# Gate half of a gMLP projection: four seven-product pairs per group, two low parts made by an accumulating DMA

## The chip, the cores and the metric

The kernel runs on one core of a Trainium2 chip. The time is the device time of one execution in microseconds (us). Four of the core's engines matter here: TensorE (PE in the profile) for matmuls, VectorE (DVE) and ScalarE (ACT) for elementwise work, and GpSimd (POOL). SyncE (SP) has a queue from which DMAs are issued; POOL has one too. Each engine runs its own instructions in a fixed order and waits on semaphores for the others.

## The reference

The reference is a two-layer trunk on an input of 256 rows by 2048 columns in float32: a gated MLP mixer (gMLP), a feed-forward part, a latent attention, another feed-forward part, each followed by a layer norm. The change lies in the first matmul of the first mixer, in the half of its columns that becomes `v`:

```python
z = jax.nn.gelu(x @ w_in)          # x: 256 x 2048, w_in: 2048 x 12288
u, v = jnp.split(z, 2, axis=-1)    # v: 256 x 6144
v = layer_norm(v, ln_g, ln_b)
```

## The kernel before

**High and low parts.** Every float32 operand is split into two tiles of a matmul format of reduced precision (`F32R`): a high part, the operand rounded to that format, and a low part, what is left. A product of two operands then takes three matmuls: high by high, low by high, and high by low (`prod_b`, L280). The high part of a weight is a cast on ACT, the low part a subtraction on DVE (L104 and L105, or `_cast`, L111, with L112 and L113).

**Groups and pairs.** The `v` half (loop at L593) computes 6144 columns in six groups of 1024. A group goes through the 2048 rows of the weight in eight pairs of 128-row blocks. The weights of one pair and one group are a chunk: a tile of 128 partitions by 2048 floats (1 MB), loaded by one DMA from SP (`_load`, L75). The 256 rows of `x` are two blocks as well, so a pair is a 2 x 2 by 2 x 2 block product, with blocks of 512 columns.

- An ordinary pair (`Banks.eight`, L337) makes the eight block products, 8 x 3 = 24 matmuls with 512 columns. Its chunk is of the kind "wide": one cast and one subtraction, 2048 wide each.
- A seven-product pair (`Banks.seven`, L344) uses a scheme with seven block products of sums of blocks, 21 matmuls. Its chunk is of the kind "seven" (`_seven`, L115): three sums on DVE (tile `ts`, L119, one instruction 1024 wide and two 512 wide), then casts and subtractions for the weight (`wh`, `wl`, 1536 wide) and for the sums (`th`, `tl`, 1536 and 512 wide). The sums of `x` (tile `xc`) are made once, by `combine` (L206) during group 0, which has wide pairs alone, and kept for the groups after.

Which pair comes when and which is of which kind stands in `V_PAIRS` and `V_SEVEN` (L49 and L50). Groups 1 to 5 have three seven-product pairs each, 2, 3 and 4, at positions 1, 4 and 6 of the group's order (positions count from 0).

**End of a group.** Four of the sums of a seven-product group lie in banks of their own. After the last seven-product pair `rest` (L354) folds them: a copy of bank p1 on ACT (L359), then u, u3, w and d on DVE (L360 to L363). After the group's last pair four additions (L616) join them with the other four banks, four gelus on ACT follow (L617), and, in the group after, four squares for the statistics of the layer norm (L590).

**Feed and order.** `Feed` hands the chunks out in order. Each `next` (L139) first calls `ahead` (L131), which splits chunks until two beyond the one asked for are split, and loads two further ones. All chunk tiles, raw ones and parts, live in one pool of 22 buffers of 8 KB per partition ("big", L152); a tile's first instruction waits until the last user of its buffer is done. The `v` tiles of finished groups, the parts of `x` and two tiles with the `xc` are in the same pool. The program text gives only the dependencies and a priority: when the kernel is built, a scheduler lays down the order of the instructions on each engine and which buffer each tile gets. That order can be read from the built program, of the kernel before and of the changed one.

Of the kernel before, what the change touches and what calls it, by code (L numbers as in the profile page):

```python
# [12 lines left out]
ALU = mybir.AluOpType  # L13
# [32 lines left out]

V_PAIRS = [[0, 1, 2, 3, 4, 5, 6, 7]] + [[0, 2, 1, 5, 3, 6, 4, 7]] * 5  # L49
V_SEVEN = [()] + [(2, 3, 4)] * 5  # L50


def halves(n_k):
# [12 lines left out]
class Feed:  # L66
# [24 lines left out]
    def _split(self):  # L91
        i = self.split
        cols, kind = self.chunks[i][1:]
        raw = self.raw.pop(i)
        if kind == "seven":
            self.parts[i] = self._seven(i, raw)
            self.split += 1
            return
        hi = self.pool.tile([P, 2048], F32R, tag="big", name=f"wh{i}")
        lo = self.pool.tile([P, 2048], F32R, tag="big", name=f"wl{i}")  # L100
        step = 512 if i == 0 else cols if kind == "wide" and i > 2 else 1024 if cols == 2048 else cols // 2
        for o in range(0, cols, step):
            c = slice(o, o + step)
            self.nc.scalar.copy(hi[:, c], raw[:, c])  # L104
            self.nc.vector.tensor_tensor(lo[:, c], raw[:, c], hi[:, c].bitcast(F32), ALU.subtract)  # L105
            if i == 0 and o == step:
                self.between[1]()
        self.parts[i] = (hi, lo)
        self.split += 1
# [20 lines left out]

    def ahead(self, n_load, n_split):  # L131
        while self.split < min(n_split, len(self.chunks)):
            if self.loaded == self.split:
                self._load()
            self._split()
        while self.loaded < min(n_load, len(self.chunks)):
            self._load()
# [9 lines left out]
def trunk(ctx: ExitStack, tc: tile.TileContext, x, xT, gm_in, gm_wout, ffn_up, ffn_dn,  # L147
# [19 lines left out]
    chunks = []  # L167
    n_up = ffn_up.shape[1]
    for g in range(6):
        for p in V_PAIRS[g]:  # L170
            chunks.append((gm_in[8 * g + p], 2048, "seven" if p in V_SEVEN[g] else "wide"))
    chunks += [(gm_in[i], 2048, "") for i in range(48, gm_in.shape[0])]

    def back(w, n_k):
# [101 lines left out]
    def x_parts(xs, k, b):  # L276
        t = xs[k // 4]
        return (t[:, k % 4, b * P : (b + 1) * P], t[:, k % 4, S + b * P : S + (b + 1) * P])
# [314 lines left out]
    for gi in range(6):  # L593

        acc = Banks(f"v{gi}", DIRECT if gi == 0 else DIRECT + OWN if gi % 2 else OWN + DIRECT)
        rest = (None,) * 4
        for c, p in enumerate(V_PAIRS[gi]):
            a = [[x_parts(xhl, 2 * p + j, b) for j in range(2)] for b in range(2)]
            got = feed.next()
            if p in V_SEVEN[gi]:  # L600
                acc.seven(a, xc[p], *got)
                if p == V_SEVEN[gi][-1]:
                    rest = acc.rest()
            else:
                acc.eight(a, *got)
            if gi == 0 and p in V_SEVEN[1]:
                x4 = xraw[p // 2]
# [70 lines left out]
    for gi in range(12):  # L678
        acc = [bank(f"u{gi}_{f}") for f in range(4)]
        for c in range(4):  # L680
            hi, lo = feed.next()
# [136 lines left out]
    for c in range(6):  # L818
        hi, lo = feed.next()
# [33 lines left out]
    for c in range(2):  # L853
        hi, lo = feed.next()
# [109 lines left out]
    for hf in range(2):  # L964
        acc = [[bank(f"vv{hf}_{b}_{f}") for f in range(2)] for b in range(2)]
        for c in range(2):
            hi, lo = feed.next()
# [20 lines left out]
    for t in range(3, H + LAG):  # L988
        k = t - LAG
        if k >= 0:  # L990
            if k % 2 == 0:
                hi, lo = feed.next()
# [22 lines left out]
    for c in range(8):  # L1015
        left = 7 - c
        hi, lo = feed.next(splits=2 if left > 5 else 3 if left > 2 else 4, loads=2 if left > 2 else 1)
# [107 lines left out]
```

## Time and profile before

| | |
|---|---|
| time, median of 3 runs | 2501.7 us (2501.2 to 2503.17) |
| the profiled execution | 2504.94 us, with a span of 2503.2 us from first to last instruction |
| granted TensorE clock of that execution | 0.997 |

In the rows of the profile "us" are microseconds; a line such as L105 is that of the kernel before. Tile names are given without their numbers. In a row of a timeline the two first numbers are the start and the length, and brackets at the end hold the idle time of the engine just ahead of the instruction and what ended it. PE matmuls are pipelined: a row's length is longer than the step from one matmul to the next, so the step is taken from pieces of the chain of several matmuls.

### The profile page before, as it was taken

The page shows a single profiled execution, that of the slowest core. Times are in us where ns is not written, and L with a number is a line of the kernel's source. Part 1 is how long each engine was busy: PE and PEld are TensorE (multiplying, and loading weights), DVE is VectorE, ACT ScalarE, POOL GpSimd, SP SyncE. Part 2 cuts the span into 40 slices and gives each one's busy share as a digit, 9 for nine tenths or more (in the row PEclk, how much of TensorE's full clock was granted, in tenths as well). Part 3 has the DMA queues.
Part 4 walks back from the last instruction along what each step waited for, and adds up shares of the span by engine and source line. Part 5 has one row for each costly group of instructions (what it writes and reads, how often), then busy time and mean ns, then how long its engine had stood idle before and what let it go on. Part 6 is the DMA issues. An engine that isn't in the chain of part 4 may idle for free.

```text
span 2503.2 us, 32484 instructions
## 1 busy us (share of the span) xinstructions
PE 2484.7 (99%) x13066; PEld 2138.5 (85%) x13066; DVE 1840.0 (74%) x2439; ACT 1335.0 (53%) x1763; POOL 2.9 (0%) x17
## 2 busy tenths in 40 slices
PE   9999999999999999999999999999999999999998
PEld 7888888888887888888888888988888888888886
DVE  6887866678787767666778887756686676668796
ACT  6565644445464546545655564565365555546553
POOL 0000000000000000000000000000000000000000
PEclk9999999999999999999999999999999999999999
DMA  7555554556566555555546674444555455555654
GB/s 276 214 190 202 202 177 161 184 192 204 187 207 252 188 182 202 185 180 176 195 156 202 217 269 157 156 143 178 183 205 183 165 206 178 182 180 172 214 203 168
DMA packets 86310, 480.19 MB, mean 192 GB/s; under 512 B 7696, under 2 KB 8336, under 8 KB 46608
## 3 DMA queue, kind: packets, MB, share of 16 engines
q1 hardware_dynamic: 86160, 478.13, 54.2%
q8 instruction: 102, 1.67, 0.3%
q14 instruction: 48, 0.39, 0.0%
HBM read 476.00 MB, written 2.10 MB: 191 GB/s over the span
## 4 chain that ended last, share of the span: by engine, by line
PE 98%; DVE 1%; ACT 0%; DMA 0%; issue 0%; SPq 0%; DVEq 0%; ACTq 0%
PE up L164 36%; PE u L164 11%; PE dn_q L164 9%; PE dn_p L164 6%; PE v_q L164 5%; PE wo_q L164 5%; PE v_p L164 3%; PE mo L164 3%; PE dn_e L164 3%; PE wo_p L164 3%; PE wo_e L164 2%; PE upf L164 2%; PE v_e L164 2%; PE mkv L164 1%; PE qn L164 1%; PE kn L164 1%
## 5 line engine op out<-in xcount | busy, mean ns | idle before, releaser
L105 DVE TENSOR_TENSOR wl<-raw,wh 128x1024 fp32r<-128x1024 f32 (+3 forms) x664 | 929.3, 1424 | 218.7 <-ACT wh L104 161.4
L104 ACT CAST wh<-raw 128x1024 fp32r<-128x1024 f32 (+3 forms) x664 | 786.4, 1215 | 341.1 <-DVE wl L105 125.2
L164 PE MATMUL up<-xhl,wh 128*128 128x512 f32 x2624 | 610.7, 390 | 0.0
L164 PEld LDWEIGHTS up<-xhl,wh 128*128 128x128 f32 x2624 | 487.4, 188 | 97.7
L164 PEld LDWEIGHTS up<-xhl,wl 128*128 128x128 f32 x2624 | 325.8, 192 | 6.4
L164 PE MATMUL up<-xhl,wl 128*128 128x256 f32 x2624 | 328.1, 283 | 0.0
L164 PE MATMUL u<-xhl,wh 128*128 128x512 f32 x768 | 183.8, 393 | 0.3 <-DVE h_u L309 0.2
L164 PEld LDWEIGHTS u<-xhl,wh 128*128 128x128 f32 x768 | 141.3, 188 | 30.8 <-PE s L164 2.1
L112 ACT CAST th<-ts 128x1536 fp32r<-128x1536 f32 x90 | 93.0, 1052 | 113.7 <-DVE ts L119 84.1
L113 DVE TENSOR_TENSOR tl<-ts,th 128x1536 fp32r<-128x1536 f32 x90 | 106.5, 1219 | 13.1 <-ACT th L112 12.2
L164 PEld LDWEIGHTS u<-xhl,wl 128*128 128x128 f32 x768 | 95.6, 192 | 2.0
L164 PE MATMUL u<-xhl,wl 128*128 128x256 f32 x768 | 96.7, 283 | 0.0
L112 ACT CAST wh<-raw 128x1536 fp32r<-128x1536 f32 x45 | 66.7, 1482 | 46.9 <-DMA raw<-in_ffn_dn_dram 13.2
L164 PE MATMUL wo_q<-wh,woa 128*128 128x512 f32 x288 | 88.9, 389 | 0.0
L113 DVE TENSOR_TENSOR wl<-raw,wh 128x1536 fp32r<-128x1536 f32 x45 | 78.8, 1752 | 6.3 <-PE dn_q L164 2.8
L164 PE MATMUL mo<-wh,oT 128*128 128x512 f32 x256 | 82.8, 404 | 0.0
L164 PE MATMUL v_q<-wh,xhl 128*128 128x512 f32 x264 | 82.0, 392 | 0.0
L164 PE MATMUL dn_q<-wh,dn0a 128*128 128x512 f32 x248 | 76.5, 389 | 0.0
L164 PE MATMUL dn_q<-wh,dn1a 128*128 128x512 f32 x248 | 76.3, 389 | 0.0
L309 DVE TENSOR_TENSOR h_0a<-up,lo_0a 128x256 f32<-128x256 f32 x41 | 17.2, 420 | 74.2 <-ACT lo_0a L307 74.1
L309 DVE TENSOR_TENSOR h_1a<-up,lo_1a 128x256 f32<-128x256 f32 x41 | 17.2, 420 | 73.3 <-ACT lo_1a L307 73.3
L164 PEld LDWEIGHTS wo_q<-wh,woa 128*128 128x128 f32 x288 | 54.1, 188 | 11.2
(490 smaller groups left out, 3847.7 us busy)
## 6 DMA issues: line engine op xcount, KB each, us to landing
raw<-in_ffn_up_dram SPq DMA_DIRECT2D x172, 1024.0 KB, 4.7
raw<-in_gm_in_dram SPq DMA_DIRECT2D x93, 1024.0 KB, 4.7
raw<-in_ffn_dn_dram SPq DMA_DIRECT2D x84, 1024.0 KB, 5.3
raw<-in_gm_wout_dram SPq DMA_DIRECT2D x48, 1024.0 KB, 5.3
raw<-in_ml_out_dram SPq DMA_DIRECT2D x16, 1024.0 KB, 4.8
raw<-in_ml_b_dram SPq DMA_DIRECT2D x14, 1024.0 KB, 4.8
raw<-in_ml_kv_dram SPq DMA_DIRECT2D x5, 864.0 KB, 4.4
lng<-in_ln_rows_dram SPq DMA_DIRECT2D x4, 1024.0 KB, 8.6
```

Source lines behind the costliest of these rows:

```text
L104: self.nc.scalar.copy(hi[:, c], raw[:, c])
L105: self.nc.vector.tensor_tensor(lo[:, c], raw[:, c], hi[:, c].bitcast(F32), ALU.subtract)
L112: self.nc.scalar.copy(hi, raw)
L113: self.nc.vector.tensor_tensor(lo, raw, hi.bitcast(F32), ALU.subtract)
L164: nc.tensor.matmul(o, l, r, start=start, stop=stop, skip_group_check=True)
L309: nc.vector.tensor_tensor(h, acc[:, 0:S], lo, ALU.add)
```

## The change

In groups 1 to 5 a fourth pair, 5, becomes a seven-product pair, and pairs 1 and 6 get a new kind, "low"; the order of the pairs changes, so that seven-product pairs stand at positions 1, 3, 5 and 6, "low" ones at positions 2 and 4 and wide ones at 0 and 7. For a "low" chunk ACT writes the negated and rounded weight into the low tile; a DMA issued from POOL then adds the weight, read from memory again, to that tile, which leaves the low part; ACT casts the high part as before. The pair itself is an ordinary one with 24 matmuls. `ahead` splits a "low" chunk one chunk earlier than it otherwise would. Lines after the inserted ones move by 10 to 15.

```diff
-V_PAIRS = [[0, 1, 2, 3, 4, 5, 6, 7]] + [[0, 2, 1, 5, 3, 6, 4, 7]] * 5
-V_SEVEN = [()] + [(2, 3, 4)] * 5
+V_PAIRS = [[0, 1, 2, 3, 4, 5, 6, 7]] + [[0, 2, 1, 3, 6, 4, 5, 7]] * 5
+V_SEVEN = [()] + [(2, 3, 4, 5)] * 5
+V_LOW = [()] + [(1, 6)] * 5
...
         hi = self.pool.tile([P, 2048], F32R, tag="big", name=f"wh{i}")
         lo = self.pool.tile([P, 2048], F32R, tag="big", name=f"wl{i}")
+        if kind == "low":
+
+            self.nc.scalar.mul(lo, raw, -1.0)
+            self.nc.gpsimd.dma_start(lo, self.chunks[i][0], accum_op=ALU.add)
+            self.nc.scalar.copy(hi, raw)
+            self.parts[i] = (hi, lo)
+            self.split += 1
+            return
...
             if self.loaded == self.split:
                 self._load()
             self._split()
+
+        if self.split < len(self.chunks) and self.chunks[self.split][2] == "low":
+            if self.loaded == self.split:
+                self._load()
+            self._split()
...
         for p in V_PAIRS[g]:
-            chunks.append((gm_in[8 * g + p], 2048, "seven" if p in V_SEVEN[g] else "wide"))
+            chunks.append((gm_in[8 * g + p], 2048, "seven" if p in V_SEVEN[g] else "low" if p in V_LOW[g] else "wide"))
```

## The prediction

> **What bounds the kernel now.** I read the page first: its busy times, the chain of work that ended last, and the issues of DMAs.
>
> ```profile
> span 2503.2 us, 32484 instructions
> ...
> PE 2484.7 (99%) x13066; PEld 2138.5 (85%) x13066; DVE 1840.0 (74%) x2439; ACT 1335.0 (53%) x1763; POOL 2.9 (0%) x17
> ...
> PE 98%; DVE 1%; ACT 0%; DMA 0%; issue 0%; SPq 0%; DVEq 0%; ACTq 0%
> ...
> raw<-in_gm_in_dram SPq DMA_DIRECT2D x93, 1024.0 KB, 4.7
> ...
> lng<-in_ln_rows_dram SPq DMA_DIRECT2D x4, 1024.0 KB, 8.6
> ```
>
> TensorE sets the end: 98% of the chain is PE. So a matmul removed is time removed, as long as every weight part is in place when PE asks for it. The change touches groups 1 to 5 of the gate half alone, so the second view is the chain in order of time there, cut to two of its pieces, and the third the busy times of two groups (columns: length, then busy us of PE, PEld, DVE, ACT, POOL, the granted clock, DMA share, GB/s).
>
> ```profile
> 88.05 2.04 PE v_q L164 x9
> ...
> 129.53 2.04 PE v_q L164 x9
> ```
>
> ```profile
> 94.00:135.50 41.50, 41.50 (x185) 34.37 (x184) 36.42 (x33) 26.76 (x32) 0.00 (x0) 1.00 0.56 203
> 135.50:177.00 41.50, 41.50 (x185) 34.38 (x184) 36.98 (x35) 26.67 (x35) 0.00 (x0) 1.00 0.58 203
> ```
>
> Nine matmuls in 2.04 us are 0.2267 us each. The same piece returns after 41.48 us, and a group has 5 wide pairs of 24 matmuls and 3 seven-product pairs of 21: 183 x 0.2267 = 41.48. PE never waits here. But DVE is busy 36.4 to 37.0 of 41.5 us: whatever is put off on DVE has little room to be caught up. How much lead DVE has is the fourth view, its instructions in order of time around the end of a group.
>
> ```profile
> 86.80 0.69 DVE L360 TENSOR_TENSOR v1u<-v_p,v1p 128x512 f32<-128x512 f32 x1 [3.98 <-PE v_p L164]
> 87.40 1.22 DVE L119 TENSOR_TENSOR ts<-raw 128x1024 f32<-128x1024 f32 x1
> 88.54 0.68 DVE L361 TENSOR_TENSOR v1w<-v_q,v1u 128x512 f32<-128x512 f32 x1
> 89.14 0.68 DVE L362 TENSOR_TENSOR v1u<-v_p,v1u 128x512 f32<-128x512 f32 x1
> 89.73 0.68 DVE L363 TENSOR_TENSOR v1d<-v1w,v_p 128x512 f32<-128x512 f32 x1
> 90.33 0.68 DVE L119 TENSOR_TENSOR ts<-ts,raw 128x512 f32<-128x512 f32 x1
> 90.93 1.75 DVE L113 TENSOR_TENSOR wl<-raw,wh 128x1536 fp32r<-128x1536 f32 x1
> ...
> 93.20 2.35 DVE L113 TENSOR_TENSOR tl<-ts,th 128x1536 fp32r<-128x1536 f32 x2
> ...
> 100.65 2.29 DVE L105 TENSOR_TENSOR wl<-raw,wh 128x2048 fp32r<-128x2048 f32 x1 [0.51 <-ACT wh L104]
> 102.86 1.22 DVE L119 TENSOR_TENSOR ts<-raw 128x1024 f32<-128x1024 f32 x1
> ```
>
> At 86.80 DVE reaches the fold of the last seven-product pair (v1u) and has idled 3.98 us for PE: by then the low parts of the next two wide pairs are done. That idle time is the lead.
>
> **The change part by part.** Positions 0 to 7 are the eight pairs of a group in their order; seven-product pairs now stand at 1, 3, 5, 6, pairs with a DMA-made low part at 2 and 4, wide ones at 0 and 7.
>
> Removed on PE: one pair per group goes from 24 to 21 matmuls, 3 x 0.2267 = 0.68 us, in five groups 3.4 us (the built program has 15 matmuls fewer). This is all that PE can gain, 0.14% of the time. About 0.2%, 5 us, is what a measurement of this kernel can tell from no change.
>
> DVE, per group: a seven-product pair costs 1.22 + 2 x 0.68 + 1.75 + 2.35 = 6.7 us against 2.29 for a wide one, so +4.4; two subtractions of 2.29 go. The load stays near 37 us of a shorter group. For ACT I read its instructions in order of time.
>
> ```profile
> 91.05 1.49 ACT L112 CAST th<-ts 128x1536 fp32r<-128x1536 f32 x1 [4.40 <-DVE ts L119]
> 93.32 0.62 ACT L112 CAST th<-ts 128x512 fp32r<-128x512 f32 x1 [0.78 <-DVE ts L119]
> 93.84 1.92 ACT L104 CAST wh<-raw 128x2048 fp32r<-128x2048 f32 x1
> 96.25 0.63 ACT L617 ACTIVATE v<-v 128x512 f32<-128x512 f32 x1 [0.49 <-DVE v L616]
> ...
> 98.72 1.90 ACT L104 CAST wh<-raw 128x2048 fp32r<-128x2048 f32 x1
> 100.53 0.72 ACT L590 ACTIVATE vsq<-v,vc 128x512 f32<-128x512 f32 x1
> ...
> 102.65 0.71 ACT L590 ACTIVATE vsq<-v,vc 128x512 f32<-128x512 f32 x1
> ...
> 103.36 1.47 ACT L112 CAST wh<-raw 128x1536 fp32r<-128x1536 f32 x1
> 104.89 2.00 ACT L112 CAST th<-ts 128x1536 fp32r<-128x1536 f32 x2
> ```
>
> ACT, per group: the seven-product pair takes 1.47 + 2.00 = 3.5 against 1.9, +1.6, and the two negations take 1.9 each (as a cast of that shape): 26.7 + 5.4 = 32 of 40.8 us. No engine is over its time; what counts is the order.
>
> Moved: the order of instructions in the built kernels. Before, DVE subtracts the low parts of positions 7 and 0 ahead of the fold. After, its order is: fold u, low part of 7, folds w, u, the low part of 0 beside the fold d, then the sums ts of position 1. And on ACT the first negation stands behind the cast th of position 1, which waits for those sums. PE's own order for the last seven-product pair changes too: the bank that the fold waits for gets its last matmul as the 19th of 21, not as the 12th. So a chain begins at S, the pair's first matmul (0.04 us for each hand-over between engines, as from the end of ts at 90.33 + 0.68 to the cast at 91.05 that waits for it):
>
> Bank ready S + 18 x 0.227 + 0.39 = 4.47; DVE: u 0.60, low part 2.21 (steps from one start to the next), w, u, d 1.80, low part 2.21, ts 1.22 + 0.68; ACT: th 1.49, negation 1.91; three hand-overs 0.12: the accumulating DMA is issued at S + 16.7.
>
> PE asks for it after 21 + 24 + 24 + 21 + 4 = 94 matmuls, S + 21.31. On the way it waits for the low part of position 7: asked for after 29 matmuls, S + 6.57, there at 4.47 + 0.04 + 0.60 + 2.29 + 0.04 = 7.44, a **new wait of 0.9 us**. So PE stands at position 2 at S + 22.2, and the DMA has **5.5 us**.
>
> Call its time from issue to PE's go **A**. Position 2 waits A - 5.5. The negation for position 4 is queued on ACT behind th 0.52, the cast wh of position 2 1.81, four gelus 2.47, three squares 2.12, and casts 1.47 and 2.00, then takes 1.91 itself: 12.3 us later (I use 12.1, the steps overlapping a little), while PE has 49 matmuls, 11.1 us, between the two asks: another 1.0. In group 5 position 4's negated tile takes over the buffer of position 2's high part, so it starts only after 18 more matmuls, 4.5 us, past the first wait: 4.5 + 1.9 + 0.1 + A - 11.1 = A - 4.6 in place of 1.0. The negation, and POOL behind it, are what waits; POOL has nothing else in its queue but one memset in group 5, which waits for a load issued ahead of that pair's own. SP's queue keeps its order of loads; a buffer that it takes over from a DMA-made tile comes free with PE's last matmul on it, as any other.
>
> Group 1 has no fold ahead of its first negation: 0.9 - 0.7 = +0.2. Groups 2 to 4: 0.9 + (A - 5.5) + 1.0 - 0.7 = A - 4.3 each. Group 5: 0.9 + (A - 5.5) + (A - 4.6) - 0.7 = 2A - 9.9. One extra combine in group 0, five DVE and one ACT instruction of at most 0.7 us, stands before any lead is spent: nothing. Sum: 0.2 + 3 x (A - 4.3) + 2A - 9.9 = 5A - 22.6 for A over 5.5.
>
> **A** is shown by no row: POOL issues no DMA now. Nearest are the loads of the same megabyte (in 40 slices of 1.05 us, and their time to landing):
>
> ```profile
> GB/s 8 195 367 429 0 0 70 250 414 421 390 374 78 0 0 0 140 320 421 117 0 101 281 406 203 23 23 203 406 367 70 226 421 421 421 429 8 0 0 0
> ...
> DMA to landing us min/median/max: 4.7/4.7/6.7
> ```
>
> At some 425 GB/s the megabyte moves in 2.5 of the 4.7 us; 2.2 are fixed. Below: 4.7, if reading the old contents costs nothing. An accumulate has to fetch its destination too, a second 2.5: 7.2. DMA share is 0.56 to 0.58 of the stage, so a load of 2.5 us will usually run in the same engines: 9.7. I take **10**. Above: the slowest 1 MB row, 8.6, has 6.4 of moving; doubled, with 2.2, 15.
>
> At A = 10: 5 x 10 - 22.6 = **+27.4 us**. The profiled execution took 2504.94 us (span 2503.2, 1.7 around it), 3.2 above the median of 2501.7; with the change 2532.3 in such an execution, 2529.1 at the median. A = 5.5 gives +4.9, A = 15 +52.4; I allow 5 more there, since group 1's own DMAs, without a price here, may then come late too.
>
> [...]
>
> **The rivals.**
> *Hidden after all (not slower).* The second fetch runs beside the first and the DMA lands like a load, A = 4.7. Position 2 then waits for nothing, position 4 0.3, position 7 still 0.9: 0.5 in groups 2 to 4, 0.3 in group 5, +0.2: +2.0, 2503.7. For it: DMA engines are idle over 40% of the stage. Against it: twice the bytes. It decides at A = 5.5.
> *Faster.* If the wait at position 7 were absent too, only the 15 matmuls would remain: -3.4, 2498.3, still within 0.2%.
> *Far slower DMA.* POOL builds the transfers itself and the add runs below the speed of a copy, A = 20: 5 x 20 - 22.6 and some 10 for group 1 = +87, 2589. For it: no row excludes it; against it: the slowest 1 MB row is 8.6. [...]
> *It doesn't do what it says.* The built program has 15 matmuls fewer and 10 accumulating DMAs, so this is left only as a slow DMA, above.
>
> **How the numbers follow.** Forecast (A from 5.5 to 15) 80%, hidden 10%, far slower 8%, faster 2%. Likeliest 2529. The range goes from A = 5.5, 2506, to A = 15 with part of group 1, 2558. Slower by over 0.2% takes A over 5.5: nearly all of the forecast and the slow case, 0.87; same 0.11; faster 0.02.
>
> **What would show it.** PE waits three times in each of groups 2 to 4: for the low part of position 7 from DVE (0.9), for POOL's DMA at position 2 (A - 5.5) and at position 4 (1.0). The group's period grows from 41.5 to some 46.5, and the stages after are unchanged. The accumulating DMA's time to landing gives A directly. No wait at position 7 would show the order argument wrong; A under 5.5 the size.

## The result, and the profile after

The changed kernel takes 2542.57 us (median of 4 runs, 2540.3 to 2544.8), the kernel before beside it 2502.43 us (4 runs, 2501.2 to 2503.25): a ratio of **1.0160, 95% interval [1.0148, 1.0172]**, some 40 us slower. The profiled execution of the changed kernel took 2541.54 us with a span of 2539.4; against the profiled execution of before that is 36.2 us more span. (Before's profiled execution lay 2.5 us above the median, this one 1.0 below its own, hence 36 and 40.) Times here and below are of runs at a granted clock of 0.993 to 0.999; one run of the kernel in which POOL subtracts took 2762.7 us at a clock of 0.838 and is left out.

The page of the changed kernel: span, busy times, the group of matmuls that waited, and the ten new DMAs.

```profile
span 2539.4 us, 32507 instructions
...
PE 2493.7 (98%) x13051; PEld 2139.7 (84%) x13051; DVE 1840.7 (72%) x2459; ACT 1359.2 (54%) x1784; POOL 11.6 (0%) x27
...
L179 PE MATMUL v_q<-wl,xhl 128*128 128x512 f32 x112 | 46.6, 416 | 26.0 <-DMA wl<-in_gm_in_dram 23.6
...
wl<-in_gm_in_dram POOLq DMA_DIRECT2D x10, 1024.0 KB, 9.2
```

PE has 15 matmuls fewer and yet 9 us more of busy time. That is the first sign that something besides waiting is in the 36 us: these matmuls have a mean of 416 ns, where 389 is the usual length. The new DMAs take 9.2 us from issue to landing, twice a load's 4.7. What PE waited for, from the view of waits (us in total, times, longest):

```profile
PE v_q L179 <- DMA wl<-in_gm_in_dram: 23.6, 7, 7.4
PE v_q L179 <- DVE wl L115: 2.3, 4, 0.6
...
PE u L179 <- DVE wl L115: 1.8, 1, 1.8
...
PE u L179 <- DVE h_u L324: 0.7, 2, 0.5
```

The first two lines did not exist before; of the last two, before had 0.2 for h_u alone. Next PE's timeline in the gate half, cut to the matmuls with idle time ahead of them (in brackets), and POOL's, with the issues.

```profile
89.26 0.50 PE L179 MATMUL v_q<-wl,xhl 128*128 128x512 f32 x1 [0.58 <-DVE wl L115]
107.42 0.51 PE L179 MATMUL v_q<-wl,xhl 128*128 128x512 f32 x1 [3.09 <-DMA wl<-in_gm_in_dram]
136.13 0.50 PE L179 MATMUL v_q<-wl,xhl 128*128 128x512 f32 x1 [0.58 <-DVE wl L115]
154.33 0.50 PE L179 MATMUL v_q<-wl,xhl 128*128 128x512 f32 x1 [3.13 <-DMA wl<-in_gm_in_dram]
166.90 0.50 PE L179 MATMUL v_q<-wl,xhl 128*128 128x512 f32 x1 [1.17 <-DMA wl<-in_gm_in_dram]
182.91 0.50 PE L179 MATMUL v_q<-wl,xhl 128*128 128x512 f32 x1 [0.58 <-DVE wl L115]
201.81 0.79 PE L179 MATMUL v_q<-wl,xhl 128*128 128x512 f32 x1 [3.88 <-DMA wl<-in_gm_in_dram]
231.63 0.50 PE L179 MATMUL v_q<-wl,xhl 128*128 128x512 f32 x1 [0.58 <-DVE wl L115]
254.11 0.80 PE L179 MATMUL v_q<-wl,xhl 128*128 128x512 f32 x1 [7.41 <-DMA wl<-in_gm_in_dram]
272.42 0.70 PE L179 MATMUL v_q<-wl,xhl 128*128 128x512 f32 x1 [4.66 <-DMA wl<-in_gm_in_dram]
```

```profile
98.75 0.86 POOL L106 DMA_DIRECT2D wl<-in_gm_in_dram  x1 [37.71 <-ACT wl L105]
...
145.62 0.86 POOL L106 DMA_DIRECT2D wl<-in_gm_in_dram  x1 [34.04 <-ACT wl L105]
...
192.42 0.86 POOL L106 DMA_DIRECT2D wl<-in_gm_in_dram  x1 [33.95 <-ACT wl L105]
...
241.11 0.86 POOL L106 DMA_DIRECT2D wl<-in_gm_in_dram  x1 [35.86 <-ACT wl L105]
...
263.21 0.86 POOL L106 DMA_DIRECT2D wl<-in_gm_in_dram  x1 [17.91 <-ACT wl L105]
```

Each issue and the matmul that takes its tile give A, from issue to PE's go: 8.67, 8.71 and 9.39 at position 2 of groups 2 to 4, 13.00 in group 5, and 9.21 at position 4 of group 5. (Recorded idle time starts where the matmul before ends, 0.39 - 0.2267 = 0.16 after the next could have begun, so each wait is 0.16 longer than its bracket.)

What was not in the sum shows when the stretches behind these waits are asked for their clock (columns as in the prediction; the granted clock is the third number from the end).

```profile
109.00:112.00 3.00, 3.00 (x8) 2.32 (x8) 2.80 (x4) 3.00 (x2) 0.86 (x1) 0.50 0.61 259
...
157.00:160.00 3.00, 3.00 (x15) 2.50 (x14) 1.73 (x2) 3.00 (x5) 0.86 (x1) 1.00 0.59 153
202.00:205.00 3.00, 3.00 (x8) 2.32 (x9) 1.63 (x2) 3.00 (x3) 0.62 (x1) 0.50 0.97 377
...
254.00:257.00 3.00, 2.89 (x7) 2.31 (x8) 0.00 (x0) 0.00 (x0) 0.00 (x0) 0.50 0.97 385
```

The second row is full speed, 15 matmuls touching 3 us. In the first and third PE is as busy, with 8, at **half the clock**: from 108.7 to 112.1, 200.8 to 207.7, 248.7 to 258.9 and 272.5 to 276.0, and not behind the wait at 154.33. Counted from where PE works again, that is 3.4 + 5.9 + 4.8 + 3.4 = 17.5 us at half clock. A step there takes 0.42 us in place of 0.2267, so these 17.5 us hold some 42 matmuls, and 42 x 0.193 = 8.1 us are lost.

### The profile page after: what moved, and what is told of

Its sections match the earlier page's. It is cut to its first block, busy times and chain, and to the rows that moved or that the text cites. A ratio compares the mean times of both kernels' runs of the same rounds, so it can differ in the third digit from the quotient of the medians.

```text
span 2539.4 us, 32507 instructions
## 1 busy us (share of the span) xinstructions
PE 2493.7 (98%) x13051; PEld 2139.7 (84%) x13051; DVE 1840.7 (72%) x2459; ACT 1359.2 (54%) x1784; POOL 11.6 (0%) x27
## 3 DMA queue, kind: packets, MB, share of 16 engines
q0 software_dynamic: 1440, 10.49, 2.2%
## 4 chain that ended last, share of the span: by engine, by line
PE 86%; DVE 1%; ACT 0%; issue 0%; DVEq 0%; ACTq 0%
PE up L179 36%; PE u L179 10%; PE dn_q L179 9%; PE dn_p L179 6%; PE wo_q L179 5%; PE mo L179 3%; PE dn_e L179 3%; PE wo_p L179 3%; PE wo_e L179 2%; PE upf L179 2%; PE mkv L179 1%; PE qn L179 1%; PE kn L179 1%; PE mq L179 1%; PE vv L179 1%; PE s L179 1%
## 5 line engine op out<-in xcount | busy, mean ns | idle before, releaser
L115 DVE TENSOR_TENSOR wl<-raw,wh 128x1024 fp32r<-128x1024 f32 (+3 forms) x649 | 895.5, 1406 | 196.9 <-ACT wh L114 137.6
L114 ACT CAST wh<-raw 128x1024 fp32r<-128x1024 f32 (+3 forms) x649 | 757.3, 1198 | 329.2 <-DVE wl L115 117.5
L122 ACT CAST th<-ts 128x1536 fp32r<-128x1536 f32 x100 | 103.7, 1050 | 115.4 <-DVE ts L129 87.9
L123 DVE TENSOR_TENSOR tl<-ts,th 128x1536 fp32r<-128x1536 f32 x100 | 119.0, 1221 | 31.5 <-ACT th L122 29.9
L122 ACT CAST wh<-raw 128x1536 fp32r<-128x1536 f32 x50 | 74.0, 1479 | 50.6 <-DMA raw<-in_ffn_dn_dram 14.4
L123 DVE TENSOR_TENSOR wl<-raw,wh 128x1536 fp32r<-128x1536 f32 x50 | 87.7, 1754 | 16.5 <-ACT wh L122 12.9
L129 DVE TENSOR_TENSOR ts<-raw 128x1024 f32<-128x1024 f32 x50 | 61.1, 1221 | 36.7 <-PE v_q L179 12.0
L179 PE MATMUL v_q<-wh,xhl 128*128 128x512 f32 x224 | 72.7, 404 | 0.4 <-ACT wh L114 0.4
L179 PE MATMUL v_q<-wl,xhl 128*128 128x512 f32 x112 | 46.6, 416 | 26.0 <-DMA wl<-in_gm_in_dram 23.6
```

The lines of the kernel that those rows point to most:

```text
L122: self.nc.scalar.copy(hi, raw)
L123: self.nc.vector.tensor_tensor(lo, raw, hi.bitcast(F32), ALU.subtract)
L129: add = lambda o, a, b: self.nc.vector.tensor_tensor(o, a, b, ALU.add)
L179: nc.tensor.matmul(o, l, r, start=start, stop=stop, skip_group_check=True)
```

## The experiments

The theory: an accumulating DMA of 1 MB needs some 9 us where the order leaves it 5.5, and long waits halve PE's clock behind them. Rivals: the fourth seven-product pair overloads DVE; a DMA from POOL is slow whatever it does; the slow stretches come from the DMA's traffic and not from PE's waiting.

### The fourth seven-product pair alone

```diff
-V_LOW = [()] + [(1, 6)] * 5
+V_LOW = [()] * 6
```

> The fourth seven-product pair alone: V_LOW is empty, so pairs 1 and 6 are ordinary wide pairs again, with the low part subtracted on DVE; no DMA is issued from POOL. Theory (the accumulating DMA, issued too late, is what costs): all of the 23.6 us in which PE waited for that DMA go, with the stretches of half clock behind them, and the 15 matmuls stay away, so the kernel is 3.4 us faster than before, some 2499, if DVE keeps up. Rival (DVE cannot carry a fourth seven-product pair): its busy time becomes 36.4 + 4.4 = 40.8 us of a group of 40.8, and PE then waits for DVE's low parts; 1 us in each of five groups makes it +1.6 against before, 3 us in each +12. The waits of PE that are put down to DVE tell the two apart.

Measured: 2502.04 us against 2502.88, ratio 0.9997 [0.9988, 1.0006]: all of the 40 us is gone, and so is most of the gain. Busy times of a stretch of 47 us (a group takes 40.8), and the waits:

```profile
93.00:140.00 47.00, 47.00 (x209) 38.93 (x208) 45.55 (x44) 32.64 (x44) 0.00 (x0) 1.00 0.54 199
```

```profile
PE u L179 <- DVE h_u L324: 1.6, 2, 1.4
...
PE u L179 <- DVE wl L115: 1.2, 1, 1.2
```

PE works through the stretch without a pause while DVE is busy 45.55 of 47 us: DVE carries the fourth pair, just. The bill comes at the start of the u half, where PE waits 1.2 and 1.6 for DVE against 0.2 before: 3.4 - 2.6 = 0.8 is left. The medians differ by 0.8 too, but the interval doesn't tell that from no change.

### The low parts by DMA alone

```diff
-V_PAIRS = [[0, 1, 2, 3, 4, 5, 6, 7]] + [[0, 2, 1, 3, 6, 4, 5, 7]] * 5
-V_SEVEN = [()] + [(2, 3, 4, 5)] * 5
+V_PAIRS = [[0, 1, 2, 3, 4, 5, 6, 7]] + [[0, 2, 1, 5, 3, 6, 4, 7]] * 5
+V_SEVEN = [()] + [(2, 3, 4)] * 5
```

> The DMA-made low parts alone: order and three seven-product pairs of the kernel before, and pairs 1 and 6 (positions 2 and 5 there) with the accumulating DMA. PE has as many matmuls as before. Theory (the DMA, some 9 us from issue to PE's go, comes late whatever the number of seven-product pairs): PE waits for that DMA in groups 1 to 5 here too, 1 to 4 us in a group, so 5 to 20 us slower than before, with half clock only where a wait is over 3 us. Rival (the fourth seven-product pair and the order that it brings are the cause): no wait for the DMA, the time of before within 0.2%.

Measured: 2533.69 us, ratio 1.0126 [1.0112, 1.0140], 31 us slower, more than expected. PE's waits:

```profile
PE v_q L179 <- DMA wl<-in_gm_in_dram: 22.0, 7, 9.2
```

So the DMA costs by itself, at other positions and with DVE relieved; the rival falls. The expected 5 to 20 was too low: the DMA took longer here (12.3 us to landing in the median; why isn't shown), and half clock, expected behind waits over 3 us alone, followed one of 2.15 as well.

### The same DMA without the adding

```diff
-            self.nc.gpsimd.dma_start(lo, self.chunks[i][0], accum_op=ALU.add)
+            self.nc.gpsimd.dma_start(lo, self.chunks[i][0])
```

> The changed kernel with the DMA from POOL as a plain copy: without accum_op it writes the whole weight over the negated tile, so the low operand of pairs 1 and 6 is the weight itself and not its low part. The order on every engine and the bytes read from memory are the same. Theory (the adding, which has to fetch the old contents too, is what makes 9.2 us of the 4.7 of a load): issue to landing falls to some 4.7 to 6, position 2's wait (5.5 us of room) is gone or under 0.5 and so is the half clock; what stays is position 7's wait of 0.74 in four groups and 1 or less at position 4, so some 2 to 6 us over before. Rival (a DMA that POOL issues is slow in itself, by its issue or its queue): issue to landing stays near 9 and the time near 2542.

Measured, in a single run: 2514.89 us, with waits for this DMA of 4.1 us in all. The time to landing of the ten DMAs, here first, then in the changed kernel:

```profile
DMA to landing us min/median/max: 4.9/5.1/10.1
```

```profile
DMA to landing us min/median/max: 7.9/9.2/13.0
```

The same bytes from memory, queue and order: **5.1 as a copy, 9.2 with the add**. POOL as the issuer isn't slow (a load from SP: 4.8). The time is 12 us above before's 2502.88, where 2 to 6 were expected: waits of 0.88 and 1.94 at position 2 of groups 4 and 5 remained, the 1.94 with a stretch of half clock behind it, and the waits for DVE at position 7 and at the start of the u half are the changed kernel's.

### Half the bytes

ACT negates and the DMA adds 1024 of the 2048 columns; DVE subtracts the rest.

```diff
-            self.nc.scalar.mul(lo, raw, -1.0)
-            self.nc.gpsimd.dma_start(lo, self.chunks[i][0], accum_op=ALU.add)
+            h = slice(0, 1024)
+            self.nc.scalar.mul(lo[:, h], raw[:, h], -1.0)
+            self.nc.gpsimd.dma_start(lo[:, h], self.chunks[i][0][:, h], accum_op=ALU.add)
             self.nc.scalar.copy(hi, raw)
+            h = slice(1024, 2048)
+            self.nc.vector.tensor_tensor(lo[:, h], raw[:, h], hi[:, h].bitcast(F32), ALU.subtract)
```

> The changed kernel with the DMA-made low part for one half of each such chunk alone: ACT negates 1024 of 2048 columns, the DMA adds 0.5 MB, DVE subtracts the other half (1.22 us more, twice per group). Theory (the accumulating DMA's time goes with its bytes): of the 9.2 us from issue to landing 7.0 are moving, so half the bytes take 2.2 + 3.5 = 5.7, and the shorter negation issues it 0.9 earlier, so it has 6.4 us: position 2's wait is gone in groups 2 to 4, the waits at position 7 (0.58) stay, position 4 keeps at most 1 and group 5's position 4 some 1 to 2: 2504 to 2510. Rival (a fixed cost of an accumulating DMA, in POOL's issue or in its many packets): issue to landing stays over 8, and the time over 2525.

Measured: 2517.51 us, ratio 1.0059 [1.0045, 1.0074].

```profile
DMA to landing us min/median/max: 5.2/6.6/11.9
```

The time goes with the bytes: by the minima, 0.5 MB less saves 7.9 - 5.2 = 2.7. An estimate from these two minima: a megabyte of adding moves in 5.4 us, on 2.5 that don't go with the bytes, about twice the 2.5 that the prediction took for a load. But 2517 is above the expected 2504 to 2510. Position 2 still waited 0.81, 3.12 and 2.67 in groups 3 to 5: in group 4 the DMA had 4.5 us (issued at 180.74, asked for at 185.2) and not the 6.4 that I worked out. PE's own order accounts for most of that: in this kernel's timeline 41 matmuls of the group stand ahead of the first that takes this low part, in the changed kernel 49, so PE asks 8 x 0.2267 = 1.8 us sooner.

### PE's waits filled with matmuls that add zeros

```diff
+                for n in DIRECT:
+                    for _ in range({(2, 1): 4, (3, 1): 4, (4, 1): 4, (5, 1): 8, (5, 6): 5}.get((gi, p), 0)):
+                        mm(acc.acc[n], idle[:, 0:P], idle, False, False)
                 acc.eight(a, *got)
```

> The changed kernel with 100 more matmuls of a zero tile, which add zeros to the sums, put ahead of the DMA-made pairs at the places where PE stood waiting: 16 ahead of position 2 in groups 2, 3 and 4, 32 ahead of position 2 and 20 ahead of position 4 in group 5; 100 x 0.2267 = 22.7 us of matmuls in place of some 22 us of waiting. Theory (PE's own waiting is what halves the clock behind it): the granted clock stays near 1.00 in groups 2 to 5, the matmul step stays 0.227, and some 8 us go: about 2534, although PE has 22.7 us more to do; waits that the slow stretches had swallowed at position 4 (up to 1 us in groups 2 to 4) may come back, 2533 to 2539. Rival (the slow stretches come from something else, such as the DMA's traffic into SBUF): they stay where they were, and the time is that of the changed kernel or longer by what the fill adds.

Measured: 2528.86 us, ratio 1.0105 [1.0091, 1.0119]: 13.7 us **faster** than the changed kernel although PE has 100 matmuls more, and 4 us below the expected 2533 to 2539. The stretches that ran at 0.50:

```profile
109.00:112.00 3.00, 3.00 (x15) 2.47 (x14) 2.97 (x4) 3.00 (x3) 0.85 (x1) 1.00 0.74 309
...
202.00:205.00 3.00, 3.00 (x15) 2.49 (x14) 2.24 (x3) 2.38 (x2) 0.00 (x0) 1.00 1.03 221
```

The clock is 1.00 throughout, with the DMAs and their traffic in place (1.03 of the DMA engines in the second row). Here it is PE's own idling that halves its clock, not the traffic. The time fell by more than the half clock's 8.1 us; other waits shrank as well, for DVE's low parts from 2.3 to 0.8 us in all and for DVE at the start of the u half from 2.5 to 0.9.

### The order on DVE put back

A column of the next two low parts is copied into p1 first, so that the fold waits for these subtractions.

```diff
-        def rest(self):
+        def rest(self, after):
...
+            for j, t in enumerate(after):
+                nc.vector.tensor_copy(p1[:, j : j + 1], t[:, 0:1].bitcast(F32))
...
-                    rest = acc.rest()
+                    rest = acc.rest([feed.parts[feed.used + j][1] for j in range(2)])
```

> The changed kernel with the order on DVE put back: one column of the low part of position 7, and one of position 0 of the next group, is copied into the tile p1 ahead of the copy that fills it, so the fold cannot start before these two subtractions; all else is as in the changed kernel. Theory (the order, fold first, is what leaves the DMA only 5.5 us): the wait of 0.58 at position 7 is gone, the two subtractions of 2.21 no longer stand between the fold and the sums ts, so the DMA is issued some 4.4 us earlier after the last seven-product pair (S + 12.5 in place of S + 16.95) and has some 9 us where its issue to PE's go takes 9.2: position 2 waits 0 to 1 us in groups 2 to 4 in place of 3.1 to 3.9, with no half clock there; position 4 keeps up to 1.2, group 5's position 4 its 4.7. About 2514, 2508 to 2520. Rival (the landing is set by POOL or the DMA rings and not by when the order lets the DMA start): waits at position 2 stay over 2 us and the time over 2530.

Measured: 2523.00 us, ratio 1.0082 [1.0066, 1.0098], half of the loss gone, but 3 us above the expected 2508 to 2520. The first DMA after group 1, and waits at position 2 of groups 3 and 4:

```profile
93.95 0.86 POOL L106 DMA_DIRECT2D wl<-in_gm_in_dram  x1 [32.84 <-DMA raw<-in_gm_in_dram]
```

```profile
148.48 0.50 PE L179 MATMUL v_q<-wl,xhl 128*128 128x512 f32 x1 [2.48 <-DMA wl<-in_gm_in_dram]
...
192.57 0.50 PE L179 MATMUL v_q<-wl,xhl 128*128 128x512 f32 x1 [1.86 <-DMA wl<-in_gm_in_dram]
```

The pair begins at 82.17, so the DMA starts at S + 11.8 where the changed kernel has S + 16.9, and no wait at position 7 is left. That is the order argument. Part of the lead was lost again: the DMA took 10.9 us in the median, not 9.2 (in group 4 from 180.79 to the matmul at 192.57, 11.8), so waits of 1.9 and 2.5 stand where 0 to 1 was expected, and one of 6.25 at position 4 of group 5 where 4.7 was. The rival's sign, waits over 2 us at position 2, shows in group 3 alone, and the time stays under its 2530. DMA share in these groups is 0.74 to 0.77. That the loads running beside it stretch it is likely by that, not shown.

### Without the early split

```diff
-        if self.split < len(self.chunks) and self.chunks[self.split][2] == "low":
-            if self.loaded == self.split:
-                self._load()
-            self._split()
```

> The changed kernel without its last part: a low chunk is no longer split one chunk earlier. In the built program DVE then makes the low part of position 7 ahead of the fold, as in the kernel before, that of position 0 still behind it, and the first negation stands behind both casts th of position 1, the second one four to five instructions (some 4 us) nearer behind the first. Theory (what counts is the chain to the DMA's issue, not when the text asks for the split): 4.47 + 2.4 (fold) + 2.21 + 1.9 (sums) + 2.0 (th) + 1.9 (negation) + 0.15 = S + 15.0 in place of 16.95, no wait at position 7, 6.5 us for the DMA: position 2 waits some 2.7 in groups 2 to 4, position 4 nothing: 2513 to 2525, faster than the changed kernel. Rival (the early split is what gives the DMA its lead): without it the DMA is issued later and the time is over 2543.

Measured: 2521.73 us, ratio 1.0076 [1.0060, 1.0092], inside the expected range and 21 us faster than the changed kernel. The part of the change that was to start the DMA sooner made it later: it moved the low part of position 7 behind the fold, and the way to the first negation grew by it. Without it the DMA after group 1 starts at 96.50 (98.75 in the changed kernel; S is the same), which is S + 14.7 where 15.0 was worked out. Position 2 waits 1.40 in group 2 (3.09 in the changed kernel), 1.97 in group 3 (3.13) and 1.14 in group 4 (3.88). The DMAs also landed sooner, 8.0 us from issue in the median in place of 9.2, so the 21 us aren't the earlier start alone. A miss: position 4 of group 2, which was to wait for nothing, waits 4.43, on a DMA of 12.3 from issue to PE's go.

### One DMA-made low part per group

```diff
-V_LOW = [()] + [(1, 6)] * 5
+V_LOW = [()] + [(1,)] * 5
```

> One DMA-made low part per group instead of two: pair 1 at position 2; pair 6 at position 4 is an ordinary wide pair. In the built program DVE makes the low part of position 7 ahead of the fold again. Theory (each accumulating DMA is late by its own chain): the negation is issued so that the DMA starts at S + 4.47 + 2.4 + 2.21 + 1.9 + 1.49 + 1.91 + 0.15 = S + 14.5, PE asks at S + 21.3, so it has 6.8 us: at 9.2 from issue to PE's go position 2 waits 2.4 in groups 2 to 4, and 3 to 6 in group 5 beside the three loads there; less 0.7 per group that is +7 to +12 with some half clock: 2509 to 2516. Rival (it takes the two DMAs together, one delaying the other, to be late): one alone is in time, and the time is 2499 to 2503.

Measured: 2512.75 us, ratio 1.0041 [1.0026, 1.0056], a time inside the expected range. One alone is late too (PE waited for it four times, 6.1 us in all); two don't merely get in each other's way. The single waits were not as worked out: 1.21, 1.08 and 3.17 in groups 2 to 4 where 2.4 was expected, and 0.68 in group 5 where 3 to 6 were, so that the time agrees is in part luck.

### POOL subtracts

```diff
-            self.nc.scalar.mul(lo, raw, -1.0)
-            self.nc.gpsimd.dma_start(lo, self.chunks[i][0], accum_op=ALU.add)
             self.nc.scalar.copy(hi, raw)
+            self.nc.gpsimd.tensor_tensor(lo, raw, hi.bitcast(F32), ALU.subtract)
```

> The changed kernel with the low parts of pairs 1 and 6 subtracted by POOL itself (weight minus its high part), with no DMA and no negation; POOL stands idle otherwise. The cast of the high part takes the negation's place ahead of it, so POOL starts at about S + 16.9 and has the same 5.5 us. Theory (the lead of 5.5 us decides, whoever makes the low part): no run here shows how long POOL takes for 128 x 2048; DVE takes 2.3. Up to 5.5 us the waits at position 2 are gone and the time is 2503 to 2510; at 9 it is the changed kernel's, 2535 to 2545; DVE's own subtractions may grow longer where both work at once. Rival (the DMA's bytes, which the subtraction doesn't move, matter by crowding the loads): the time falls below 2515 even where POOL takes longer than 5.5 us.

Measured: 2530.78 us (three runs), ratio 1.0112 [1.0091, 1.0132]. The timeline of POOL, DVE and PE where it starts:

```profile
97.73 4.89 POOL L106 TENSOR_TENSOR wl<-raw,wh 128x2048 fp32r<-128x2048 f32 x1 [33.14 <-ACT wh L105]
...
98.73 4.46 DVE L122 TENSOR_TENSOR tl<-ts,th 128x512 fp32r<-128x512 f32 x1
...
103.24 0.80 PE L178 MATMUL v_q<-tl,xhl 128*128 128x512 f32 x1 [2.65 <-DVE tl L122]
```

POOL takes 4.9 us, within the 5.5, and position 2 does wait no longer, as the lead of 5.5 has it (PE's own wait at position 1, below, gives it more time still). But the time of 2503 to 2510 expected for that case is missed by 20 us. The expectation said that DVE's subtractions may grow longer and gave that no price: a DVE subtraction of 0.69 us lasts 4.46 while POOL works, and PE waits 2.65 for it at position 1, in each of four groups (10.6 us in all). PE also waits for POOL's second subtraction of a group (4.6 to 5.6 us long), at position 4 of groups 3 to 5, and 17.1 us in and behind these waits run at half clock. The waits for POOL:

```profile
PE v_q L178 <- POOL wl L106: 3.6, 3, 2.2
```

POOL began 1.0 us ahead of that DVE subtraction, which ended 0.6 us after POOL did. Why it lasts so long isn't shown beyond this.

### Four seven-product pairs in groups 1 to 4

```diff
-V_PAIRS = [[0, 1, 2, 3, 4, 5, 6, 7]] + [[0, 2, 1, 3, 6, 4, 5, 7]] * 5
-V_SEVEN = [()] + [(2, 3, 4, 5)] * 5
-V_LOW = [()] + [(1, 6)] * 5
+V_PAIRS = [[0, 1, 2, 3, 4, 5, 6, 7]] + [[0, 2, 1, 3, 6, 4, 5, 7]] * 4 + [[0, 2, 1, 5, 3, 6, 4, 7]]
+V_SEVEN = [()] + [(2, 3, 4, 5)] * 4 + [(2, 3, 4)]
+V_LOW = [()] * 6
```

> No low parts by DMA; four seven-product pairs in groups 1 to 4, and group 5 with the order and the three seven-product pairs of the kernel before. Theory (with four in all five groups the 3.4 us of removed matmuls were given back by PE's waits for DVE at the start of the u half, 1.2 for wl and 1.6 for h_u against 0.2 before, where DVE came late out of group 5): 12 matmuls fewer, 12 x 0.2267 = 2.7, and no such waits: 2.7 us faster than before, a ratio of 0.9989. Rival (the waits at the start of the u half come from the fourth pair of any group, or the gain is lost elsewhere): within 1 us of before.

Measured: 2500.23 us (11 runs) against 2501.70 (14 runs), ratio 0.9991 [0.9983, 1.0000]. The waits at the start of the u half are back to before's:

```profile
PE u L179 <- DVE h_u L324: 0.2, 1, 0.2
```

The forecast ratio of 0.9989 lies within the interval, but so, at its upper end, does no change. By the time alone the rival (within 1 us of before) isn't excluded; it is the waits at the start of the u half that bear the theory out. The median is the lowest of these kernels.

## Why the prediction was right, and what its sum lacked

**The order.** Shown. In group 1 the last seven-product pair starts at 81.81 (S). DVE's timeline behind it:

```profile
86.32 0.69 DVE L375 TENSOR_TENSOR v1u<-v_p,v1p 128x512 f32<-128x512 f32 x1 [0.89 <-PE v_p L179]
86.92 2.28 DVE L115 TENSOR_TENSOR wl<-raw,wh 128x2048 fp32r<-128x2048 f32 x1
...
90.32 2.28 DVE L115 TENSOR_TENSOR wl<-raw,wh 128x2048 fp32r<-128x2048 f32 x1
...
94.37 0.69 DVE L129 TENSOR_TENSOR ts<-ts,raw 128x512 f32<-128x512 f32 x1
```

Before, DVE idled 3.98 us ahead of the fold with both low parts done; now it reaches the fold 4.51 after S (4.47 + 0.04 forecast) with both still to do. The DMA is issued at 98.75, S + 16.9 (16.7 forecast), and PE asks some 0.2 later than forecast as well. Putting the order back moved the DMA forward by 5.1 us and took half of the loss away.

**The new wait at position 7.** Four times 0.58 recorded, 0.74 in fact; 0.9 forecast. (In group 5 two matmuls of the next stage, brought forward, fill it.) From one to the next the group's period is 46.87, 46.78 and 48.72; some 46.5 was forecast. That agreement is luck: the forecast figure takes the 0.7 of the removed matmuls off twice (by the sum it is 41.5 + 10 - 4.3 = 47.2), and with the measured A's the sum gives 45.9, 45.9 and 46.6; the rest is mostly half clock.

**The waits for the DMA.** With the measured A in the prediction's own terms, A - 5.5 gives 3.2, 3.2, 3.9 and 7.5 at position 2, where PE waited 3.25, 3.29, 4.04 and 7.57 (the brackets and 0.16); group 5's position 4 should wait 9.21 - 4.6 = 4.6 and waited 4.82. The buffer taken over there is thus borne out, to 0.2 us.

**A.** Taken as 10; 8.7 to 9.4, and 13.0 in group 5, whose first DMA runs beside three loads, two of them (wT and bsum) for the next stage; that these stretch it isn't shown. The reason given, a second fetch of the destination, fits: copy 5.1, half the bytes 6.6, whole 9.2. That it is this fetch, and not the adding itself, that takes the time isn't shown either: the page counts 10.49 MB for the ten DMAs, each megabyte once.

**The sum** with the measured A's: 0.2 + (4.4 + 4.4 + 5.1) + (0.9 + 7.5 + 4.6 - 0.7) = 26.4, where 27.4 was forecast for A = 10. That these two are so near is partly luck: 10 was 0.6 to 1.3 too much at four places and 3.0 too little at the fifth. Measured are 36.2. What it lacked or mis-sized:

- **The half clock, +8.1**, is the step that failed: the prediction gave every matmul 0.2267 us whatever stood ahead of it. In the slow stretches a step takes 0.42. The filled kernel shows that it is the waiting which does it.
- "The stages after are unchanged" failed by 2.3: the u half starts with 2.5 us of waits for DVE in place of 0.2. The kernel with the fourth pair alone has them too, and the one with group 5 as before has not.
- Position 4 was to wait 1.0 in groups 2 to 4: 1.33 in group 3, and nothing in 2 and 4, where the slow matmuls ahead of it gave the DMA its time (-1.7). Group 1's wait of 0.24 (0.40) there adds 0.4; position 7, four times 0.16 less and nothing in group 5, takes 1.5 off; the five waits by A were longer than their terms by 0.6 in all.
- Matmuls near a wait have longer steps, 0.34 right behind one: some +2.6 over groups 1 to 5, by the starts in PE's timeline.
- The profiled execution of before was itself slow at its start. Its group 1 begins at 52.53 us, that of the changed kernel at 50.64: -1.9. There PE waited 1.7 us for ACT in group 0 (0.4 in the changed kernel), and half clock followed:

```profile
PE v_p L164 <- ACT wh L104: 1.7, 1, 1.7
```

```profile
9.00:12.00 3.00, 3.00 (x8) 2.35 (x8) 1.64 (x5) 1.82 (x4) 0.00 (x0) 0.50 1.01 404
```

26.4 + 8.1 + 2.3 - 1.7 + 0.4 - 1.5 + 0.6 + 2.6 - 1.9 = 35.3 of 36.2; 0.9 stays unplaced. So the direction and the mechanism of the waits were right, and the size was 9 us short in the profiled execution (2541.5 for 2532.3), 13 in the median (2542.6 for 2529.1). The result lies within the range because that allowed A up to 15, not because the half clock was seen. (The top of the range is 2501.7 + 52.4 + 5 = 2559, not 2558.)

**The gain.** 3.4 us was the most that PE could win. Without the DMAs the medians show 0.8 of it, with group 5 as before 1.5; neither interval excludes no change.

## What to carry to other kernels

An engine that idles for TensorE isn't spare time: DVE's 3.98 us ahead of the fold were the lead of everything behind it, and a step moved past the fold costs that lead. A unit of work given to an idle queue must be priced from its own issue to the consumer's go, against the time that the built order leaves there; here 9 against 5.5. And where TensorE is the bound, a wait of a few us can cost more than itself; here 8.1 us of half clock came on top of 23.6 of waiting for the DMA.

## What the runs showed of the hardware

**Half clock came in steps.** The slow stretches of the changed kernel last 3.4, 6.9, 10.2 and 3.4 us, whole multiples of 3.4, and begin at 108.7, 200.8, 248.7 and 272.5: behind the first by 27, 41 and 48 times 3.41. The first beginning, in slices of 0.1 us:

```profile
108.60:108.70 0.10, 0.10 (x2) 0.06 (x1) 0.10 (x1) 0.10 (x2) 0.00 (x0) 1.00 0.58 246
108.70:108.80 0.10, 0.10 (x2) 0.09 (x1) 0.10 (x1) 0.10 (x1) 0.00 (x0) 0.53 1.56 655
```

So the half clock of this kernel began and ended at points whole multiples of 3.41 us apart. PE's idle time, counted between two neighbouring points of this kind (each run's own, by its half clock), fits the waits that seemed not to agree: 3.09 us of waiting at 107.42 had 2.1 between two points and was followed by half clock; 3.13 at 154.33 was split 1.9 and 1.2 and was not. Where POOL subtracts, four equal waits of 2.64 us had 2.0, 1.9, 2.3 and 2.3 between two points; the second alone stayed at full clock. Below 2.0 the runs differ: the copy from POOL went slow at 1.9 too, before's first stretch at 1.7, while 1.7 between two points in the kernel with the DMAs alone (the wait that ends at 150.44) did nothing. So something besides these idle times may enter. No run set the phase on purpose.

**POOL's issue.** An accumulating DMA keeps POOL 0.86 us, a plain copy 0.53 (medians of ten each), of the 9.2 and 5.1 us to landing.
